# Hybrid decoder layer: the normalised attention output in a tile of its own, and GpSimd's product with the PSUM copy first of five

## The chip, the cores and the metric

The kernel runs on one core of one Trainium2 chip. The metric is the device time of one execution in microseconds. Three runs of the kernel before gave 1129.52, 1127.29 and 1125.67 us; the median is 1127.29 us.

## The reference

One decoder layer on x (1024 positions, 1024 columns, float32): one input projection into 3072 columns, four heads of differential attention, a gated short convolution, an output projection, layer norm, a gated feed-forward block with 2816 hidden columns, and a second layer norm. The change lies in what ends each attention head:

```python
a = p[:, :, 0] - lam * p[:, :, 1]                  # two causal softmaxes, in 128-query blocks
o = jnp.einsum('bhqk,bhkd->bhqd', a.astype(vt.dtype), vt)
...
o = o * lax.rsqrt(jnp.mean(jnp.square(o), axis=-1, keepdims=True) + RMS_EPS)
o = o * attn_norm_g.astype(jnp.float32) * (1.0 - lam_init)
...
cat = jnp.concatenate([attn_out, conv_out], axis=-1)
return jnp.einsum('bsc,cd->bsd', cat, w_out)
```

## The kernel before

Products that need float32 accuracy are split: a cast `hi` on ScalarE (line 63), the rest `lo = src - hi` on VectorE (line 64), and three matmuls on TensorE (lines 72 to 74). After the value projection the attention runs head by head, `attention(h)` for h = 0 to 3. Each head projects its q and k, then goes over four chunks c of 256 queries, each with two blocks `qi` of 128 queries, so block i = 2c + qi has (i + 1) x 128 keys. A block has, for each of the two softmaxes, score matmuls (lines 441 to 443), the row maximum on VectorE (line 444) and the exponential on ScalarE (line 448), and then the combination of the two (line 456 on ScalarE, line 457 on VectorE). `spread` of that block comes in the program at the start of the next block: it transposes the weights (line 408), splits them into `pa`, and after the second block of a chunk multiplies them with v into the PSUM tile `o`, which line 419 copies into `osb` on ScalarE.

`normalise` for a chunk comes one block later still, at `RMS_AT` (c, 1), after the exponentials of that block; for the last chunk of a head it comes in the next head, or after the last head. It squares `osb` on VectorE, splits the square into `sqh` and `sql`, takes the mean over the head's 128 rows with two matmuls against `ones` into `mq`, makes y = (mean square + eps)^(-1/2) on ScalarE (logarithm and exponential), and refines and applies it in five GpSimd operations: two products, a scale-and-add with the columns `gm` and `gp`, and two more products. The last writes over `osb`, and SP's queue sends `osb` to `cat_d[h]` in DRAM, from where the output projection reads it after the four heads.

All tiles of `normalise` come from the pool `at`, in which a tag without a count has one buffer. `sq` and `me` share the tag "sq", `sql` and `y` the tag "sql"; `sqh` and `osb` have tags of their own. A tile that takes a buffer waits until the tile before it in that buffer has been used for the last time.

Each head is followed in the program by parts of the short convolution (`conv_1` to `conv_3`, lines 481 to 501), whose projections (tiles X and Z, `a`, `s`, `w`, `u`) have nothing to do with the attention and fill its gaps. The order in which an engine's queue holds its instructions is not that of the source: it is laid down when the kernel is built, by a planner that gives each engine, among the instructions whose operands and buffers it takes to be ready, the one that stands first in the program. On the chip each queue runs in that order, and an instruction whose semaphore has not come holds up all behind it in its queue.

Of the kernel before, what the change touches and what calls it, by code (L numbers as in the profile page):

```python
# [8 lines left out]
F32 = mybir.dt.float32  # L9
# [3 lines left out]
ALU = mybir.AluOpType  # L13
# [3 lines left out]
P = 128  # L17
# [11 lines left out]
QC = 256  # L29
# [17 lines left out]
def layer_kernel(ctx: ExitStack, tc: tile.TileContext, x, xt, w_in, w_v, lam, vecs, w_out, ln, w_up, w_down, out):  # L47
    nc = tc.nc
    V, A, T, G = nc.vector, nc.scalar, nc.tensor, nc.gpsimd
    SQ = nc.sync  # L50

    def pool(name, stack=None, side=None, space=None, **kw):
        args = dict(name=name, bufs=1, reuse_waits="tile")
        if space is not None:
            args["space"] = space
        if side is not None:
            args["side"] = side
        return (stack or ctx).enter_context(tc.tile_pool(**args))

    def split(hi, lo, src, scale=None, eng=None):  # L60

        if scale is None:
            A.copy(hi, src)  # L63
            (eng or V).tensor_tensor(lo, src, hi.bitcast(F32), op=ALU.subtract)  # L64
        else:
            A.mul(hi, src, scale)
            V.scalar_tensor_tensor(lo, src, scale, hi.bitcast(F32), op0=ALU.mult, op1=ALU.subtract)
# [79 lines left out]
    cat_d = [dram.tile([P, S], F32, name=f"cat_d{k}") for k in range(8)]  # L147
# [172 lines left out]
    at = pool("at", ab, side="right")  # L320
# [30 lines left out]
    def normalise(h, c, osb):  # L351
        sq = at.tile([P, QC], F32, name="sq", tag="sq")
        V.tensor_tensor(sq, osb, osb, op=ALU.mult)
        sqh = at.tile([P, QC], F32R, name="sqh", tag="sqh")
        sql = at.tile([P, QC], F32R, name="sql", tag="sql")
        split(sqh, sql, sq)
        mq = p_pv.tile([P, 512], F32, name="mq", tag="pv", bufs=1)
        T.matmul(mq[:, :QC], ones, sqh, start=True, stop=False)
        T.matmul(mq[:, :QC], ones, sql, start=False, stop=True)

        me = at.tile([P, QC], F32, name="me", tag="sq")
        A.activation(me, mq[:, :QC], AF.Identity, bias=epsc)
        y = at.tile([P, QC], F32, name="y", tag="sql")
        A.activation(y, me, AF.Ln)
        A.activation(y, y, AF.Exp, scale=-0.5)  # L365
        G.tensor_tensor(me, me, y, op=ALU.mult)  # L366
        G.tensor_tensor(me, me, y, op=ALU.mult)
        G.tensor_scalar(me, me, gm, gp, op0=ALU.mult, op1=ALU.add)
        G.tensor_tensor(y, y, me, op=ALU.mult)
        G.tensor_tensor(osb, y, osb, op=ALU.mult)  # L370
        SQ.dma_start(cat_d[h][:, c * QC:(c + 1) * QC], osb)

    def attention(h):

# [27 lines left out]
        def spread(c, qi, pm, pa):  # L402
            i, nkb = 2 * c + qi, 2 * c + 2
            for j0 in range(0, i + 1, 4):
                nj = min(4, i + 1 - j0)
                tp = p_tr.tile([P, 4, P], F32, name="tp", tag="tr", bufs=1)
                for j in range(nj):
                    T.transpose(tp[:, j, :], pm[0][:, (j0 + j) * P:(j0 + j + 1) * P], ident)
                g = pa[j0 // 4]
                split(g[:, 0, 0:nj, qi * P:(qi + 1) * P], g[:, 1, 0:nj, qi * P:(qi + 1) * P], tp[:, :nj, :])  # L410
            if qi == 0:
                return
            o = p_pv.tile([P, 512], F32, name="o", tag="pv", bufs=1)
            for j in range(nkb):
                qs = slice(P if j == nkb - 1 else 0, QC)
                mm3(o[:, qs], vh[:, j, :], vl[:, j, :], pa[j // 4][:, 0, j % 4, qs], pa[j // 4][:, 1, j % 4, qs],
                    j == 0, j == nkb - 1, skip_group_check=True)
            osb = at.tile([P, QC], F32, name="osb", tag="osb")
            A.copy(osb, o[:, :QC])
            rms.append(lambda: normalise(h, c, osb))  # L420
# [272 lines left out]
    def operand(src, which, i, tail=False, eng=None):  # L693
        if tail and not (which == "T" and i < HK - NTAIL + RT):
            v = ep.tile([P, 2, 512], F32R, name=f"{which}{i}", tag="ra", bufs=NF - NKEEP)
        else:
            v = e0.tile([P, 2, 512], F32R, name=f"{which}{i}", tag="ring", bufs=RING[0])
        split(v[:, 0, :], v[:, 1, :], src, eng=eng)
        return v
# [121 lines left out]
    def add(x_, y_, op, out=None):  # L821
        if out is None:
            out = ep.tile([P, 512], F32, name="tm", tag="r", bufs=4)
        V.tensor_tensor(out, x_, y_, op=op)
        return out
# [33 lines left out]
    for j in range(HK + 2):  # L859
        if j < HK:  # L860
            op = ready.pop(0) if ready else (operand(a11[j], "S", j), operand(b11[j], "T", j))
            for t in range(4):
                mm_row(X, op, t, j == 0, j == HK - 1)
        if j >= 2:
            i = j - 2
            op = (operand(add(a21[i], a22[i], ALU.add), "S", i),
                  operand(add(b12[i], b11[i], ALU.subtract), "T", i))
# [91 lines left out]
```

## Time and profile before

| what | value |
|---|---|
| median of three runs | 1127.29 us |
| the profiled execution's own time | 1129.07 us |
| its span, first to last instruction | 1127.3 us |
| mean granted TensorE clock | 0.991 |
| TensorE matmul busy | 1084.9 us, 96% |
| VectorE busy | 906.4 us, 80% |
| ScalarE busy | 522.5 us, 46% |
| GpSimd busy | 147.6 us, 13% |
| chain that ended last: PE, DVE, ACT, POOL, DMA | 71%, 15%, 5%, 3%, 3% |

Engines are named as the profile names them: PE is TensorE's matmuls, PEld its weight loads, DVE VectorE, ACT ScalarE, POOL GpSimd, SP the queue that issues the transfers. A matmul's recorded end is modelled, and matmuls overlap, so a busy PE is not yet PE at its peak. The four heads take the span from about 85 to 380 us.

### The profile page before, as it was taken

What the parts mean: (1) busy time and instruction counts of PE and PEld (TensorE: products, weight loads), DVE (VectorE), ACT (ScalarE), POOL (GpSimd) and SP (SyncE); (2) the same over time, 40 slices, a digit from 0 to 9 for tenths busy, and PEclk for the clock granted to TensorE, in tenths of its full rate; (3) what the DMA queues carried; (4) which work ended last, traced back from release to release, by engine and by line L of the source; (5) the groups of instructions that cost most, each with busy time, mean ns of one, the idle gap of its engine ahead of it and who ended that gap; (6) DMA issues with size and microseconds to landing.
All of it is one profiled execution on the core that took longest, in us unless ns stands there. A gap on an engine that the chain in (4) does not pass through costs nothing.

```text
span 1127.3 us, 13854 instructions
## 1 busy us (share of the span) xinstructions
PE 1084.9 (96%) x4940; PEld 873.8 (78%) x4940; DVE 906.4 (80%) x1393; ACT 522.5 (46%) x980; POOL 147.6 (13%) x182
## 2 busy tenths in 40 slices
PE   7999999999999999879999999999999999999996
PEld 6777877876768888668888888888888887788885
DVE  7678898689787688998967676777777599997797
ACT  6357586386675333445433334333333333444540
POOL 0002213013031224760000000000000000000102
PEclk9999999999999999999999999999999999999998
DMA  7421201301206754423232212131312295111111
GB/s 267 150 94 43 85 25 52 115 21 52 75 29 197 279 177 159 154 75 113 94 112 70 99 59 109 57 113 57 112 56 93 78 383 220 38 66 38 46 67 75
DMA packets 50421, 118.53 MB, mean 105 GB/s; under 512 B 5040, under 2 KB 18480, under 8 KB 50352
## 3 DMA queue, kind: packets, MB, share of 16 engines
q1 hardware_dynamic: 50352, 117.64, 29.7%
q8 instruction: 39, 0.64, 0.2%
q14 instruction: 30, 0.25, 0.1%
HBM read 90.88 MB, written 26.74 MB: 104 GB/s over the span
## 4 chain that ended last, share of the span: by engine, by line
PE 71%; DVE 15%; ACT 5%; POOL 3%; DMA 3%; issue 2%; SPq 0%; POOLq 0%; DVEq 0%; ACTq 0%
PE X L74 8%; PE X L72 8%; PE X L73 8%; PE Z L74 5%; PE Z L73 5%; PE Z L72 5%; PE dx L73 2%; PE dx L74 2%; PE dx L72 2%; PE op L74 2%; PE op L73 2%; PE op L72 2%; DVE a L64 2%; PE dz L74 2%; PE dz L72 2%
## 5 line engine op out<-in xcount | busy, mean ns | idle before, releaser
L64 DVE TENSOR_TENSOR a<-s,a 128x512 fp32r<-128x512 f32 x118 | 85.3, 724 | 45.3 <-ACT a L63 44.3
L63 ACT CAST a<-s 128x512 fp32r<-128x512 f32 x118 | 73.3, 623 | 94.5 <-PE X L74 43.0
L63 ACT CAST a<-w 128x512 fp32r<-128x512 f32 x106 | 65.9, 623 | 87.3 <-PE X L74 40.4
L64 DVE TENSOR_TENSOR a<-w,a 128x512 fp32r<-128x512 f32 x102 | 72.3, 710 | 22.6 <-ACT a L63 22.2
L63 ACT CAST T<-b 128x512 fp32r<-128x512 f32 x66 | 40.6, 621 | 68.4 <-PE dz L74 33.9
L73 PE MATMUL dx<-T,S 128*128 128x512 f32 x176 | 69.0, 392 | 1.2 <-DVE T L64 1.2
L74 PE MATMUL dx<-T,S 128*128 128x512 f32 x176 | 68.5, 389 | 0.0
L72 PE MATMUL dx<-T,S 128*128 128x512 f32 x176 | 66.0, 391 | 0.0
L64 DVE TENSOR_TENSOR T<-b,T 128x512 fp32r<-128x512 f32 x66 | 45.0, 685 | 16.3 <-ACT T L63 16.3
L74 PE MATMUL op<-wo,cl 128*128 128x512 f32 x128 | 51.2, 400 | 3.2 <-DVE cl L64 3.2
L444 DVE TENSOR_REDUCE nm<-sc 128x1 f32<-128x128 f32 (+5 forms) x64 | 47.5, 750 | 7.7 <-PE sc L443 7.3
L709 POOL MEMSET gs<- 128x2 f32 x22 | 2.2, 99 | 379.6 <-DVE t L728 379.6
L73 PE MATMUL dz<-T,S 128*128 128x512 f32 x132 | 51.8, 393 | 0.0
L74 PE MATMUL dz<-T,S 128*128 128x512 f32 x132 | 51.5, 390 | 0.0
L72 PE MATMUL op<-wo,ch 128*128 128x512 f32 x128 | 51.3, 401 | 0.0
L448 ACT ACTIVATE p<-sc,nm 128x128 f32<-128x128 f32 (+5 forms) x64 | 47.6, 745 | 7.2 <-DVE p L457 4.1
L73 PE MATMUL op<-wo,ch 128*128 128x512 f32 x128 | 50.8, 397 | 0.0
L72 PE MATMUL dz<-T,S 128*128 128x512 f32 x132 | 48.4, 393 | 0.5 <-ACT T L63 0.5
L729 ACT ACTIVATE t<-t 128x1024 f32<-128x1024 f32 x22 | 23.4, 1062 | 51.9 <-DVE t L728 51.9
L441 PE MATMUL sc<-k,q 128*128 128x512 f32 (+2 forms) x96 | 37.1, 394 | 7.1 <-ACT p L448 6.1
L366 POOL TENSOR_TENSOR me<-me,y 128x256 f32<-128x256 f32 x16 | 12.5, 783 | 236.0 <-ACT y L365 236.0
L63 ACT CAST wo<-wo_r 128x512 fp32r<-128x512 f32 x40 | 24.4, 619 | 40.9 <-PE op L74 37.8
(314 smaller groups left out, 3374.9 us busy)
## 6 DMA issues: line engine op xcount, KB each, us to landing
w<-in_w_up SPq DMA_DIRECT2D x44, 512.0 KB, 3.2
b<-in_w_down SPq DMA_DIRECT2D x44, 256.0 KB, 6.9
w<-in_w_in SPq DMA_DIRECT2D x20, 512.0 KB, 3.4
wo_r<-in_w_out SPq DMA_DIRECT2D x20, 512.0 KB, 4.8
act_d<-act SPq DMA_DIRECT2D x19, 512.0 KB, 2.6
ra<-act_d SPq DMA_DIRECT2D x19, 512.0 KB, 7.0
v_d<-vs SPq DMA_DIRECT2D x16, 256.0 KB, 2.7
vhl<-v_d SPq DMA_DIRECT2D x8, 512.0 KB, 4.6
```

Source lines behind the costliest of these rows:

```text
L63: A.copy(hi, src)
L64: (eng or V).tensor_tensor(lo, src, hi.bitcast(F32), op=ALU.subtract)
L72: T.matmul(ps, lh, rh, start=first, stop=False, **kw)
L73: T.matmul(ps, lh, rl, start=False, stop=False, **kw)
L74: T.matmul(ps, ll, rh, start=False, stop=last, **kw)
L366: G.tensor_tensor(me, me, y, op=ALU.mult)
L441: T.matmul(sc[:, bs], q2[m][:, qs], k2[m][:, bs], start=True, stop=False)
L444: V.tensor_reduce(nm[:, m:m + 1], sc[:, :n], axis=AX.X, op=ALU.max, negate=True)
L448: A.activation(pt[:, :n], sc[:, :n], AF.Exp, bias=nm[:, m:m + 1], accum_out=sm[:, m:m + 1])
L709: G.memset(gs[:, 0:2], 0.0)
L729: A.activation(t_, t_, AF.Silu)
```

## The change

`normalise` gets one more tile, `on`, in the buffer of tag "sqh". The product of `y` with `osb` is made first, into `on`; the refinement of `me` follows; the last product multiplies `on` with `me`, and `on` is what is sent to DRAM. The count of operations is the same, and so are the kinds; the scale-and-add, third of the five before, is now the fourth. `osb` is read for the last time by the first GpSimd operation, `y` by the third, `me` by the fifth.

```diff
         A.activation(y, y, AF.Exp, scale=-0.5)
+        on = at.tile([P, QC], F32, name="on", tag="sqh")
+        G.tensor_tensor(on, y, osb, op=ALU.mult)
         G.tensor_tensor(me, me, y, op=ALU.mult)
         G.tensor_tensor(me, me, y, op=ALU.mult)
         G.tensor_scalar(me, me, gm, gp, op0=ALU.mult, op1=ALU.add)
-        G.tensor_tensor(y, y, me, op=ALU.mult)
-        G.tensor_tensor(osb, y, osb, op=ALU.mult)
-        SQ.dma_start(cat_d[h][:, c * QC:(c + 1) * QC], osb)
+        G.tensor_tensor(on, on, me, op=ALU.mult)
+        SQ.dma_start(cat_d[h][:, c * QC:(c + 1) * QC], on)
```

## Rows read from the trace of the kernel before

**Rows 1.** The page: busy us of each engine, share of the span, instructions.

```profile
PE 1084.9 (96%) x4940; PEld 873.8 (78%) x4940; DVE 906.4 (80%) x1393; ACT 522.5 (46%) x980; POOL 147.6 (13%) x182
```

**Rows 2.** Chain that ended last, in head 0: start us, duration us, what.

```profile
99.48 0.75 POOL me L366
...
104.70 1.87 DMA cat_d<-osb
```

**Rows 3.** Waits of ScalarE, 85 to 380 us: total us, times, longest.

```profile
ACT osb L419 <- DMA cat_d<-osb: 7.7, 5, 2.0
```

**Rows 4.** Timeline, ScalarE: start, duration us, instruction, [idle before <- releaser].

```profile
106.65 0.37 ACT L419 COPY osb<-o 128x256 f32<-128x256 f32 x1 [1.57 <-DMA cat_d<-osb]
...
108.07 0.41 ACT L63 CAST sqh<-sq 128x256 fp32r<-128x256 f32 x1
...
174.26 0.37 ACT L419 COPY osb<-o 128x256 f32<-128x256 f32 x1 [2.00 <-DMA cat_d<-osb]
...
258.66 0.37 ACT L419 COPY osb<-o 128x256 f32<-128x256 f32 x1 [1.00 <-DMA cat_d<-osb]
259.53 0.40 ACT L63 CAST sqh<-sq 128x256 fp32r<-128x256 f32 x1 [0.49 <-DVE sq L353]
...
329.61 0.37 ACT L419 COPY osb<-o 128x256 f32<-128x256 f32 x1 [1.96 <-DMA cat_d<-osb]
```

**Rows 5.** Timeline, TensorE, behind those copies.

```profile
108.24 0.50 PE L441 MATMUL sc<-k,q 128*128 128x512 f32 x1 [0.74 <-ACT p L448]
...
130.50 0.39 PE L73 MATMUL o<-pa,vhl 128*128 128x256 f32 x1 [0.72 <-DVE pa L64]
...
176.38 0.50 PE L441 MATMUL sc<-k,q 128*128 128x512 f32 x1 [1.61 <-ACT p L448]
...
259.99 0.39 PE L358 MATMUL mq<-sqh,ones 128*128 128x256 f32 x1 [0.58 <-ACT sqh L63]
...
331.72 0.50 PE L441 MATMUL sc<-k,q 128*128 128x512 f32 x1 [1.56 <-ACT p L448]
```

**Rows 6.** VectorE in head 0 (timeline), and busy us by stretch (windows).

```profile
107.22 0.29 DVE L64 TENSOR_TENSOR pa<-tp,pa 128x128 fp32r<-128x128 f32 x1 [1.32 <-ACT pa L63]
107.43 0.41 DVE L353 TENSOR_TENSOR sq<-osb 128x256 f32<-128x256 f32 x1
...
108.82 0.42 DVE L64 TENSOR_TENSOR sql<-sq,sqh 128x256 fp32r<-128x256 f32 x1
...
110.00:130.00 20.00, 19.79 (x113) 16.18 (x111) 19.94 (x30) 13.76 (x27) 9.05 (x11) 1.00 0.04 14
```

**Rows 7.** Timeline, head 0: last matmul into `o`, ScalarE's idle stretch.

```profile
100.08 0.27 PE L74 MATMUL o<-pa,vhl 128*128 128x128 f32 x1
...
103.60 0.59 ACT L63 CAST pa<-tp 128x512 fp32r<-128x512 f32 x1 [1.60 <-PE tp L408]
```

**Rows 8.** Timeline, VectorE and GpSimd side by side, heads 0, 1 and 2.

```profile
101.30 0.68 DVE L64 TENSOR_TENSOR a<-w,a 128x512 fp32r<-128x512 f32 x1
101.47 1.58 POOL L368 TENSOR_SCALAR me<-me,gm,gp 128x256 f32<-128x256 f32 x1
101.90 0.88 DVE L457 SCALAR_TENSOR_TENSOR p<-p,cc,p 128x640 f32<-128x640 f32 x1
...
169.11 1.20 POOL L368 TENSOR_SCALAR me<-me,gm,gp 128x256 f32<-128x256 f32 x1
169.12 0.92 DVE L457 SCALAR_TENSOR_TENSOR p<-p,cc,p 128x640 f32<-128x640 f32 x1
...
254.11 0.56 POOL L368 TENSOR_SCALAR me<-me,gm,gp 128x256 f32<-128x256 f32 x1
254.75 0.73 POOL L369 TENSOR_TENSOR y<-y,me 128x256 f32<-128x256 f32 x1
254.81 1.35 DVE L457 SCALAR_TENSOR_TENSOR p<-p,cc,p 128x640 f32<-128x640 f32 x1
```

**Rows 9.** Timeline, TensorE, head 2: the transposes behind L457.

```profile
256.31 0.63 PE L408 MATMUL tp<-ident,p 128*128 128x128 f32 x4 [0.72 <-DVE p L457]
```

## The prediction

> **What bounds the kernel now.** I read the page's busy times first: TensorE is at work for 96% of the span, ScalarE for 46% [rows 1]. A change on ScalarE, VectorE or GpSimd therefore gains only what takes idle time from TensorE. Next I read the chain of waits over the four attention heads (about 85 to 380 us), since only `normalise` is touched. In each head it passes once through all five GpSimd products and the transfer behind them: in head 0 from 99.48 us to the landing at 104.70 + 1.87 = 106.57 us [rows 2]. So the edited place is on the path four times. Third, who waited there: ScalarE stood 7.7 us, five times, at the copy of `o` into `osb` for that transfer [rows 3]. Four of these are the second chunk of each head, 1.57, 2.00, 1.00 and 1.96 us, 6.53 in all; the fifth is the rest, some 1.1 us [rows 4]. Fourth, what TensorE lost by it, read from TensorE's rows just behind these places: it was idle 0.74, 1.61 and 1.56 us for an exponential of L448 that stood behind the copy, and 0.58 us for the cast into `sqh`, 4.49 us together [rows 5]. In the stretch after the first of them TensorE is full (19.79 of 20 us), with VectorE at 19.94 [rows 6]; time won on the other engines there is not won in the span, unless VectorE's backlog itself stops TensorE, as it does once (0.72 us at 130.50) [rows 5].
>
> **Part 1, `osb` becomes free earlier.** Before, the next copy into `osb` had to wait for five products and the transfer. Now it waits for the first product: 99.48 + 0.75 = 100.23 us in head 0 [rows 2]. The last product of the matmuls that it copies ends at 100.35 [rows 7]. So the copy can go at once, and ScalarE has an idle stretch of 1.60 us just there, before 103.60 [rows 7] (heads 1 and 3 have one like it): the copy's 0.37 us lie in it, cost nothing, and would cost 0.37 us of ScalarE if that cover were gone.
>
> **Part 2, what takes its place.** `on` lies in the one buffer of tag `sqh`. The next chunk's cast into `sqh` must now wait until `on` has been read by its transfer, which lands when it did before: five products, the same transfer, 106.57 us. As the rows stand, the cast ran at 108.07, 1.50 us after that landing [rows 4], and with that order it would never wait. But the cast stands there only because `sq` waited for the late `osb`. With `osb` early, `sq` can run on VectorE as soon as `me`, whose buffer it takes, is read for the last time (just ahead of the transfer's issue at 104.70 [rows 2], one product later than before), and VectorE has 1.32 us idle before 107.22 [rows 6]. The order of each queue is laid down before the run, by when the planner thinks that an operand or buffer is ready. It put the copy into `osb` behind the second exponential of the head's sixth block, that is, at the time at which it thought that the transfer would be in, and it was too early by the 1.57, 2.00, 1.00 and 1.96 us that ScalarE then stood. The cast into `sqh` now depends on the same transfer and ranks ahead of the next block's exponential, so I expect it at that same place. The added wait is then worth between nothing (the cast stays behind the landing) and 2.00 us a head; I take the old waits, since the row of the old copy is the nearest. Behind the cast in the queue stand a cast of `pa` and the next exponential of L448, and TensorE's score matmul at 108.24 waits for that one, as before [rows 5]. In heads 0, 1 and 3 a cast of 0.41 us stands where a copy of 0.37 us stood, and the three gaps of TensorE (0.74, 1.61, 1.56) stay: nothing gained.
>
> Two things are gained. In head 2 TensorE waited 0.58 us for the cast itself, which came 0.87 us behind the copy (259.53 against 258.66) [rows 4, 5]; the cast now stands in the copy's place, and the gap goes: -0.58. In head 0 VectorE works without a break from 107.22 until it stops TensorE at 130.50; `sq` and `sql` (0.41 and 0.42 us) leave that stretch for the idle time ahead of it, more than the gap of 0.72 [rows 5, 6]: -0.72. Sum -1.30. Bounds for the two together: nothing, if other work slips in, and -1.30.
>
> **Part 3, the order of the five products.** It was product, product, scale-and-add, product, product; it becomes product, product, product, scale-and-add, product. No instruction is added on GpSimd, VectorE, SP or the DMA queues; `on` itself waits for no one, since the matmuls that read `sqh` are over before `y` can be made; `y` is free two products earlier, which nobody waits for. What changes is which of them stands beside VectorE's combination of the two softmaxes (L457), for which TensorE's transposes wait. On 640 columns it took 0.88 and 0.92 us beside the scale-and-add (heads 0 and 1; head 3 is like head 1), and 1.35 us beside two products (head 2) [rows 8]; the scale-and-add, in turn, took 1.58 and 1.20 us there, against 0.56 ahead of L457 in head 2. In head 2 the third product will be over when L457 starts (254.11 + 0.73 = 254.84 against 254.81), and the scale-and-add stands beside it: 1.35 falls to about 0.90, and the transposes' gap of 0.72 us with it [rows 8, 9]: -0.45. In head 1 the third operation and L457 start within 0.01 us of each other (169.11 and 169.12), and in head 3 alike. If the product goes first, L457 ends later by about a product, 0.73 us, and TensorE with it, 1.46 in both; if L457 goes first, nothing. I take the middle, +0.73, as no row decides. In head 0 another two-operand instruction of VectorE (101.30) runs directly ahead of L457 while GpSimd already stands, so I put nothing there. Part 3: +0.28, between -0.45 and +1.01.
>
> The Trainium skill (GPSIMD Engine Reference, 1. Specifications) says that GpSimd shares its SBUF interfaces with VectorE, and that the two contend where VectorE's instruction has two SBUF inputs or runs in a 2-port mode. It speaks against this change, which moves a two-input product to where L457 runs. It does not say which side waits; if VectorE did in heads 0, 1 and 3, at the 0.45 us by which the rows of L457 differ, part 3 would be 3 x 0.45 - 0.45 = +0.90 and the whole -0.4 us. The rows bear out that there is contention, and that the scale-and-add, not VectorE, stood in those three heads.
>
> **Sum.** -1.30 + 0.28 = -1.0 us. The profiled execution took 1129.07 us (span 1127.3 and 1.8 around it), so it would take 1128.1. It is 1.78 us above the median of the runs, 1127.29; applied to the median, 1126.3 us.
>
> **Rivals.** *A, the forecast: the wait moves to the cast into `sqh`.* 1126.3; its own range is 1123 to 1130, since a new order of ScalarE's and VectorE's queues also moves fill work of the convolution projections by a few tenths of a microsecond in each of some ten places. Chance 0.48.
>
> *B, the wait is gone.* The cast into `sqh` is put behind the exponential, as it stands in heads 0, 1 and 3 now, and the transfer has landed by then. All four gaps go: -4.49, then -0.72 in head 0 and +0.28 from part 3: -4.9, or 1122.4. For it: the 1.50 us between landing and cast today. Against: the cast's rank ahead of that exponential. Chance 0.28.
>
> *C, slower: VectorE stands too.* The buffer of `sq` is now given back by the fifth product instead of the fourth, and the planner's view of the products is too short by what contention adds (5.22 us from 99.48 to 104.70, where five at 0.73 would be 3.65) [rows 2, 8]. If `sq` is put ahead of the next block's reduction and of a `pa` subtraction, these, and the transposes that wait for `pa`, stand behind it. At most VectorE would stand as long as ScalarE did, 6.53 us over the heads; about half lies beside ScalarE's own wait. Price +3.3, 1130.6 (at most 1133.8). It decides from where `sq` reaches the head of VectorE's queue before 104.70. Against: VectorE is seldom idle earlier. Chance 0.18.
>
> *D, nothing changes.* The planner keeps its order and what moves is hidden behind TensorE: 1127.3. For it: TensorE's 96%. Against: the copy ranks first where it is ready. Chance 0.06.
>
> **How the numbers follow.** 0.3% is 3.4 us, about what a measurement of this kernel tells from no change: faster means below 1123.9, slower above 1130.7. Faster: 0.27 of B and 0.04 of A's tail, 0.31. Slower: 0.12 of C and 0.08 of A's and D's tails, 0.20. Same: 0.49. The range takes in B with a microsecond and a half below it and C to its price: 1120.8 to 1131.0.
>
> **What would show it.** Right: the four waits of `osb` for a transfer are gone, and ScalarE stands 1 to 2 us at the cast into `sqh` for the transfer of `on`, once a head, with TensorE's gaps of 0.7 to 1.6 us still behind it. B: neither wait, and no such gaps. C: VectorE idle ahead of `sq`, released by GpSimd's last product. Part 3: L457 on 640 columns at 0.9 us in head 2, and its length in heads 1 and 3. The prediction is wrong if the copy into `osb` does not move, if the cast meets no wait, or if stretches after 380 us change.

## The result and the profile after

| | before | changed |
|---|---|---|
| median, six runs each | 1126.65 us | 1134.72 us |
| profiled execution, its span | 1129.07, 1127.3 us | 1135.76, 1134.0 us |
| first score matmul to first matmul of the output projection | 288.6 us | 295.6 us |

The ratio is 1.0058, 95% interval 1.0042 to 1.0073: slower by 0.6%, or 6.5 us (8.1 between the two medians), outside the range that was forecast. All of it arises in the four heads, 7.0 us there against 6.7 in the span of the profiled executions. The page of the changed kernel (its first lines and the shares of its chain) shows TensorE busy for 4.9 us longer with the same 4940 instructions, and GpSimd for 5.9 us longer [rows 1]. It does not say why: its row of the clock has 9 tenths in every slice.

```profile
span 1134.0 us, 13870 instructions
## 1 busy us (share of the span) xinstructions
PE 1089.8 (96%) x4940; PEld 878.9 (78%) x4940; DVE 902.4 (80%) x1393; ACT 522.7 (46%) x980; POOL 153.5 (14%) x182
...
PE 71%; DVE 13%; ACT 5%; DMA 4%; POOL 3%; issue 2%; SPq 0%; POOLq 0%; DVEq 0%; ACTq 0%
```

The waits of the heads in the changed kernel (total us, times, longest) show the forecast mechanism. `osb` waits for no transfer any more, only for its own matmuls [rows 3]; the cast into `sqh` does wait for one, four times, once a head. TensorE now stands behind that cast itself, and VectorE stands at `sq` for the fifth product.

```profile
ACT sqh L63 <- DMA cat_d<-on: 8.4, 4, 2.5
ACT osb L420 <- PE o L74: 7.6, 4, 2.4
...
PE mq L358 <- ACT sqh L63: 7.0, 4, 2.1
...
DVE sq L353 <- POOL on L371: 3.8, 4, 1.1
```

Head 1 in the changed kernel, ScalarE's timeline: the copy goes at 169.63, 4.6 us earlier than before [rows 4], in what had been idle time, and the cast then stands 2.49 us.

```profile
169.63 0.36 ACT L420 COPY osb<-o 128x256 f32<-128x256 f32 x1
169.88 0.60 ACT L63 CAST pa<-tp 128x512 fp32r<-128x512 f32 x1
172.97 0.40 ACT L63 CAST sqh<-sq 128x256 fp32r<-128x256 f32 x1 [2.49 <-DMA cat_d<-on]
```

TensorE's timeline at the same place. Its queue has one matmul of the fill work after the scores, and then the product of `sqh`: 2.07 us idle. Read the starts behind it: from 174.31 to 174.73 one 512-column matmul takes 0.42 us, from 177.54 to 177.77 it takes 0.23.

```profile
170.88 0.47 PE L73 MATMUL Z<-xb_22l,a 128*128 128x512 f32 x1
173.43 0.39 PE L358 MATMUL mq<-sqh,ones 128*128 128x256 f32 x1 [2.07 <-ACT sqh L63]
...
174.31 0.63 PE L72 MATMUL Z<-xb_22h,a 128*128 128x512 f32 x1
174.73 0.63 PE L73 MATMUL Z<-xb_22l,a 128*128 128x512 f32 x1
...
177.54 0.40 PE L74 MATMUL Z<-xb_22h,a 128*128 128x512 f32 x1
177.77 0.40 PE L72 MATMUL X<-xb_t3h,a 128*128 128x512 f32 x1
```

The windows of that stretch (PE, PEld, DVE, ACT, POOL busy; the third column from the right is the granted clock) say why: behind the idle stretch the clock is at 0.50 of 2.4 GHz, that is 1.2 GHz, while TensorE is busy throughout.

```profile
168.00:171.30 3.30, 3.18 (x20) 2.19 (x18) 2.18 (x4) 2.18 (x5) 2.91 (x2) 1.00 0.10 38
171.30:173.40 2.10, 0.06 (x1) 0.00 (x0) 0.75 (x2) 0.40 (x1) 0.00 (x0) 1.00 0.67 133
174.00:177.20 3.20, 3.20 (x10) 2.62 (x9) 3.09 (x5) 2.76 (x6) 0.00 (x0) 0.50 0.15 58
178.00:181.00 3.00, 3.00 (x18) 2.50 (x17) 2.46 (x4) 2.39 (x5) 1.88 (x3) 1.00 0.00 0
```

The kernel before had its gap of 1.61 us at this place [rows 5], and its windows show the clock at full speed on both sides:

```profile
174.70:176.40 1.70, 0.09 (x2) 0.03 (x1) 1.44 (x4) 1.70 (x5) 0.00 (x0) 1.00 0.59 239
176.40:180.00 3.60, 3.60 (x19) 2.95 (x20) 3.46 (x6) 3.15 (x6) 0.71 (x1) 1.00 0.00 0
```

The same happens in heads 2 and 3 of the changed kernel (idle 2.12 and 2.04 us, clock low from 262.6 and 334.3):

```profile
262.64:266.05 3.41, 3.33 (x9) 2.71 (x10) 3.35 (x7) 2.78 (x7) 0.00 (x0) 0.50 0.28 111
334.32:337.73 3.41, 3.41 (x9) 2.67 (x9) 2.65 (x6) 2.32 (x7) 0.00 (x0) 0.50 0.00 0
```

In head 0 the gap is 0.75 us and the clock stays.

### The profile page after: what moved, and what is told of

The parts are those of the page before. It is cut to its first block, busy times and chain, and to the rows that moved or that the text cites. A ratio compares the mean times of both kernels' runs of the same rounds, so it can differ in the third digit from the quotient of the medians.

```text
span 1134.0 us, 13870 instructions
## 1 busy us (share of the span) xinstructions
PE 1089.8 (96%) x4940; PEld 878.9 (78%) x4940; DVE 902.4 (80%) x1393; ACT 522.7 (46%) x980; POOL 153.5 (14%) x182
## 4 chain that ended last, share of the span: by engine, by line
PE 71%; DVE 13%; ACT 5%; DMA 4%; POOL 3%; issue 2%; SPq 0%; POOLq 0%; DVEq 0%; ACTq 0%
PE X L72 8%; PE X L74 8%; PE X L73 8%; PE Z L74 5%; PE Z L73 5%; PE Z L72 5%; PE dx L73 2%; PE dx L74 2%; PE dx L72 2%; PE op L74 2%; PE op L72 2%; PE op L73 2%; DVE a L64 2%; PE dz L74 2%; PE dz L72 2%
## 5 line engine op out<-in xcount | busy, mean ns | idle before, releaser
L64 DVE TENSOR_TENSOR a<-s,a 128x512 fp32r<-128x512 f32 x118 | 83.0, 705 | 44.4 <-ACT a L63 43.3
L367 POOL TENSOR_TENSOR on<-y,osb 128x256 f32<-128x256 f32 x16 | 14.6, 911 | 242.3 <-ACT y L365 200.6
```

What stands on the lines that cost most here:

```text
L367: G.tensor_tensor(on, y, osb, op=ALU.mult)
```

## The stage's account

The windows from the first score matmul to the first matmul of the output projection, one row each of the kernel before, the changed one, and two of the experiments (e3, a buffer of its own for `on`; e4, more matmuls in the gap):

```profile
81.00:369.60 288.60, 276.94 (x1422) 216.61 (x1423) 239.27 (x418) 194.32 (x419) 63.78 (x78) 1.00 0.21 72
```

```profile
80.20:375.80 295.60, 281.85 (x1422) 221.98 (x1423) 234.66 (x418) 194.76 (x419) 69.23 (x78) 0.98 0.21 71
```

```profile
79.60:359.60 280.00, 276.06 (x1423) 217.25 (x1424) 234.95 (x418) 193.60 (x419) 67.89 (x78) 1.00 0.23 75
```

```profile
80.30:379.70 299.40, 285.46 (x1446) 222.38 (x1447) 236.60 (x418) 195.15 (x419) 67.95 (x78) 1.00 0.21 69
```

TensorE's idle time is the length less its busy time: 11.7 us before, 13.8 changed. TensorE's busy time grew from 276.9 to 281.9 us for the same 1422 matmuls; 2.1 + 4.9 are the 7.0. In the changed kernel 10.2 us of the stage ran at 1.2 GHz, where 512-column matmuls followed each other at 0.42 us instead of 0.23, so nearly half of that, at most 5.1 us, is lost: that is the growth of the busy time. The same account for all kernels of this study, length and idle time from the kernel's own window row, the time at 1.2 GHz from the stretches that its trace shows at a clock of 0.50:

| kernel | length | idle | at 1.2 GHz | length - idle - half of that |
|---|---|---|---|---|
| before | 288.6 | 11.7 | 0 | 276.9 |
| changed | 295.6 | 13.8 | 10.2 | 276.7 |
| e1 order only | 291.7 | 13.5 | 3.4 | 276.5 |
| e2 tile only | 292.3 | 13.5 | 3.4 | 277.1 |
| e3 own buffer | 280.0 | 3.9 | 0 | 276.1 |
| e4 keep busy | 299.4 | 13.9 | 0 | 285.5, with 24 matmuls more |
| e5 square in PSUM | 288.1 | 9.0 | 6.8 | 275.7 |
| e6 two of osb | 282.3 | 6.4 | 0 | 275.9 |
| e7 own buffer, old order | 287.7 | 10.0 | 3.4 | 276.0 |
| e8 keep one | 296.5 | 13.9 | 6.8 | 279.2, with 6 matmuls more |
| e9 before, square in PSUM | 303.6 | 18.9 | 17.1 | 276.2 |
| e10 buffers exchanged | 294.4 | 14.7 | 6.8 | 276.3 |
| e11 on in sql's buffer | 288.6 | 11.0 | 0 | 277.6 |

The last column is TensorE's busy time less half of the time at 1.2 GHz. Apart from e4 and e8, whose added matmuls are in it, it is the same within 2 us, while the lengths differ by 24. So TensorE's idle time and the time at 1.2 GHz are what the stage's length is made of; where VectorE, ScalarE or GpSimd wait counts only as far as it makes these.

## The experiments

All times are medians, ratios are against the kernel before on the same chip (medians 1127.3 to 1127.7 us).

**e1, the order alone.**

```diff
+        G.tensor_tensor(osb, y, osb, op=ALU.mult)
         G.tensor_tensor(me, me, y, op=ALU.mult)
...
-        G.tensor_tensor(y, y, me, op=ALU.mult)
-        G.tensor_tensor(osb, y, osb, op=ALU.mult)
+        G.tensor_tensor(osb, osb, me, op=ALU.mult)
```

> The kernel before (1126.7 us) with the first product ahead of the refinement, but in place: it writes over osb, the last product too, and osb is sent. No new tile. Theory W (the loss of 8 us is the wait of the cast into sqh for the transfer of on, once a head, with what it does to TensorE): osb waits for the transfer as before, no cast into sqh waits, 1125 to 1129. Theory O (the loss is the new order of the products beside VectorE's two-operand instructions): most of the loss is here too, 1131 to 1135. Theory P (any new order of the queues costs it): undecided, anything between.

Measured 1131.02 us, ratio 1.0032 (1.0019 to 1.0044): at the lower end of O's range and outside W's, with 3.6 us of loss, about half of what the change lost. The trace shows the slower instructions that O had put down. VectorE's combination of the softmaxes (L457) took 1.34 and 1.37 us in heads 0 and 1, for 0.88 and 0.92 before, and 1.37 in head 3; in head 2 the scale-and-add took 2.22 us for 0.56 [rows 8], and ScalarE then stood 2.80 us for the transfer behind it, for 1.00 [rows 4]:

```profile
ACT osb L419 <- DMA cat_d<-osb: 13.6, 6, 4.0
...
101.66 1.34 DVE L457 SCALAR_TENSOR_TENSOR p<-p,cc,p 128x640 f32<-128x640 f32 x1
...
169.65 0.74 POOL L368 TENSOR_TENSOR me<-me,y 128x256 f32<-128x256 f32 x1
169.69 1.37 DVE L457 SCALAR_TENSOR_TENSOR p<-p,cc,p 128x640 f32<-128x640 f32 x1
...
256.32 2.22 POOL L369 TENSOR_SCALAR me<-me,gm,gp 128x256 f32<-128x256 f32 x1
261.38 0.37 ACT L419 COPY osb<-o 128x256 f32<-128x256 f32 x1 [2.80 <-DMA cat_d<-osb]
```

The whole wait for the transfer was 7.7 us before [rows 3]; the clock fell once in the stage, behind 2.39 us idle in head 2. What the planner's new order of the queues adds to this was not separated.

**e2, the tile alone.**

```diff
-        G.tensor_tensor(osb, y, osb, op=ALU.mult)
+        on = at.tile([P, QC], F32, name="on", tag="sqh")
+        G.tensor_tensor(on, y, osb, op=ALU.mult)
```

> The kernel before with only the target of the last product changed: it goes to on, in the buffer of tag sqh, and on is sent; the products keep their old order, so osb is free after the fifth product, not the first. Theory W: the cast into sqh is held by the same landing, but the copy into osb comes only 1.9 us ahead of it, so the cast waits 0.5 to 2 us and TensorE loses 0 to 2 us at mq in each head: 1127 to 1134, slower where a clock stretch at half speed shows behind such a gap. Theory O: the order is the old one, so 1125 to 1128. Theory P: undecided.

1132.94 us, 1.0045 (1.0031 to 1.0058), in the range of W, but for the most part not by W's way: the cast waited for the transfer three times, 0.8 us at most. ScalarE stood 3.6 us once at `osb` for the fifth product, and the clock fell once in the stage, behind the 2.45 us that TensorE then stood in head 0:

```profile
104.50 0.37 ACT L420 COPY osb<-o 128x256 f32<-128x256 f32 x1 [3.57 <-POOL on L371]
105.82 0.50 PE L442 MATMUL sc<-k,q 128*128 128x512 f32 x1 [2.45 <-ACT p L449]
```

Either part alone loses; the two losses do not add up (3.6 + 5.1 against 6.5 from the ratios).

**e3, a buffer of its own for `on`.** The room for it comes from the raw square, put into the unused half of the bank of `mq`; the tags of `me` and `y` move up.

```diff
+        mq = p_pv.tile([P, 512], F32, name="mq", tag="pv", bufs=1)
+        sq = mq[:, QC:]
...
-        me = at.tile([P, QC], F32, name="me", tag="sq")
+        me = at.tile([P, QC], F32, name="me", tag="sql")
...
-        y = at.tile([P, QC], F32, name="y", tag="sql")
+        y = at.tile([P, QC], F32, name="y", tag="sqh")
...
-        on = at.tile([P, QC], F32, name="on", tag="sqh")
+        on = at.tile([P, QC], F32, name="on", tag="on")
```

> The changed kernel (1134.7 us) with a buffer for on that nobody else takes. The room for it comes from the raw square, which goes to the unused half of the PSUM tile mq; me then takes the buffer of sql, y that of sqh. Theory W: neither osb nor sqh waits for a transfer, TensorE is not idle 2 us ahead of mq, its clock keeps 2.4 GHz through the four heads, 1120 to 1125, below the kernel before. Theory O: the order of the products is that of the changed kernel, so 1131 to 1135. Theory P: anything, most likely above 1127.

1117.57 us, 0.9917 (0.9903 to 0.9930): better than W expected, and the fastest kernel of the study, 0.8% below the kernel before. Theory O by itself is out: the products stand in the order of the changed kernel, and the scale-and-add of head 2 takes 2.23 us here too, but no write waits for its transfer. Head 1 in its timeline: the cast and the product of `sqh` follow without a wait.

```profile
169.66 0.33 SPq L372 DMA_DIRECT2D cat_d<-on  x1
...
170.19 0.38 ACT L63 CAST sqh<-mq 128x256 fp32r<-128x256 f32 x1
...
171.74 0.28 PE L358 MATMUL mq<-sqh,ones 128*128 128x256 f32 x1
```

The cast begins 0.53 us behind the issue of the transfer; in the changed kernel it had to wait until that had landed.

**e4, matmuls into the gap.**

```diff
+        if c == 1:
+            for _ in range(3):
+                T.matmul(mq[:, :QC], ident, sq, start=True, stop=True)
```

> The changed kernel with three matmuls more (ident times the raw square, into mq, thrown away) ahead of the first matmul into mq, in the second chunk of each head only, that is, in the gap of TensorE. The wait for the transfer stays. They take 1.3 us a head where there is no gap. Theory W with the clock as half of the loss: the gap falls below 1 us, the clock stays at 2.4 GHz in heads 1 to 3, and about 1.7 us a head come back: 1128 to 1131. If the clock were without weight and only the wait counted: no change or slower, 1134 to 1138. Theories O and P: 1134 to 1140.

1137.47 us, 1.0093 (1.0079 to 1.0106): a miss of the forecast gain, and a time in the range put down for a clock without weight, so the time alone does not speak for the clock. The clock did stay at 2.4 GHz in all four heads (table), but the added matmuls took 285.5 - 276.7 = 8.8 us of TensorE, not the 5.2 that I had put (3 a head became 24 records of some 0.4 us), and TensorE's idle time stayed as it was, 13.9 us for 13.8. -5.1 + 8.8 = +3.7, and the stage grew by 3.8: the account holds, with the clock in it at the price worked out above.

**e5, the control: the square in PSUM, the wait kept.** e3 with the changed kernel's tags of `me`, `y` and `on`.

> The control for the buffer of its own (1117.6 us): the raw square goes to PSUM as there, but on stays in the buffer of tag sqh, as in the changed kernel. Theory W: the wait of the cast for the transfer is back, 1.5 to 2.5 us in each head, with TensorE idle ahead of mq and its clock falling: 1130 to 1136. If the gain of the other kernel came from the square in PSUM (theory S): 1116 to 1121.

1127.26 us, 0.9991 (0.9980 to 1.0002): a miss for W as I had put it. The wait is there, and longer than in the changed kernel:

```profile
ACT sqh L63 <- DMA cat_d<-on: 9.7, 5, 3.2
```

But TensorE stood long behind it in two heads only, 0 and 2 (2.89 and 1.80 us, each with a fall of the clock, where the cast waited 3.17 and 2.61 us). In heads 1 and 3 the cast waited 1.25 and 1.31 us, and TensorE stood 0.52 and 0.59: the wait is half of the changed kernel's there, and more of the fill work stands ahead of `mq` in its queue. So the wait in sum is not the loss; its length in each head and what TensorE has left to do during it decide, and the two were not separated. By the ratios, of the 15.9 us between the changed kernel and e3, 7.6 came with the square in PSUM and 8.3 with the buffer of its own (and the tags of `me` and `y` that go with it).

**e6, two buffers of `osb`, the old order.** The room is made as in e3.

```diff
-            osb = at.tile([P, QC], F32, name="osb", tag="osb")
+            osb = at.tile([P, QC], F32, name="osb", tag="osb", bufs=2)
```

> The kernel before with two buffers for osb and nothing moved in the order of the products; the room comes from the raw square in PSUM, me in the buffer of sql, y in that of sqh. Theory W: no instruction waits for a transfer of the attention output, 1116 to 1121, as with the buffer of its own. Theory O (part of what was gained is that GpSimd's product with osb comes first): 1121 to 1126.

1120.16 us, 0.9937 (0.9923 to 0.9951): W. No instruction waits for a transfer of the attention output.

**e7, the buffer of its own, the old order of the products.** e3 with `on` made last, from `y` and `osb`.

> The buffer of its own for on, but with the products in the order of the kernel before: osb is free after the fifth product. Theory W: no wait for a transfer; the copy into osb may wait for the fifth product, up to 1.5 us in a head: 1117 to 1123. Theory O in the sense that the new order costs 3.6 us, as it did in place: 1114 to 1116. The other way round (the new order helps once the buffer is free): 1119 to 1124.

1125.37 us, 0.9976 (0.9964 to 0.9987), by the ratios 6.6 us above e3: with the buffer free, the new order helps, the third of the cases put down, and by a little more than its range. ScalarE waits for the fifth product instead of a transfer:

```profile
ACT osb L420 <- POOL on L371: 9.9, 4, 2.8
```

**e8, one matmul into the gap, in heads 1 to 3.**

```diff
+        if c == 1 and h > 0:
+            T.matmul(mq[:, :QC], ident, sq, start=True, stop=True)
```

> The changed kernel (1134.7 us) with a single matmul more (ident times the raw square, thrown away) ahead of the first into mq, in the second chunk of heads 1 to 3, the three places where the clock fell. It adds 0.5 us a head where there is no gap, and lies in the gap of 2 us here. The wait for the transfer stays. Theory W with the clock: no stretch at 1.2 GHz in heads 1 to 3, 3 x 1.7 us come back less at most 1.5: 1129.5 to 1132. If a fall of the clock costs nothing (what is lost is made up behind it): 1134 to 1136.

1134.84 us, 1.0062 (1.0046 to 1.0078): no gain, and again a time in the range put down for a clock without weight. The gap was split (0.67 and 1.26 us in head 1), and the clock fell all the same in heads 1 and 3, but not in head 2. By the account, one fall less gives back 1.7 us and the added matmuls take 2.5, with the idle time as it was: +0.9 in all, which is what the stage grew. Two of its windows, behind the gaps of heads 1 and 2:

```profile
174.00:177.00 3.00, 3.00 (x10) 2.48 (x11) 2.97 (x7) 1.85 (x4) 0.00 (x0) 0.50 0.35 143
...
264.60:267.60 3.00, 3.00 (x16) 2.34 (x15) 3.00 (x6) 2.65 (x6) 0.00 (x0) 1.00 0.15 60
```

**e9, the kernel before with the square in PSUM.**

> The kernel before (1127.7 us) with only the raw square moved to PSUM; osb is still sent and held by its transfer, in one buffer. It is the control for two buffers of osb (1120.2). Theory W: the copy into osb waits for the transfer as before, 6 to 8 us in all; the square in PSUM is not what counts: 1124 to 1129. Theory S (the square in PSUM, which frees the buffer that me holds until the fourth product, gains by itself, as it did on the changed kernel): 1118 to 1122.

1138.66 us, 1.0099 (1.0080 to 1.0119): slower than either theory had it; on this kernel theory S is out. ScalarE's wait for the transfer is three times as long, and the stage has five stretches' worth of 3.4 us at 1.2 GHz (table). Why the square in PSUM makes that wait longer here, and gained on the changed kernel (e5), was not found. With two buffers of `osb`, and `me` and `y` moved up a tag, the same kernel is e6, 18 us faster.

```profile
ACT osb L419 <- DMA cat_d<-osb: 22.6, 7, 4.8
```

**e10, `me` and `y` exchange buffers.**

```diff
-        me = at.tile([P, QC], F32, name="me", tag="sq")
+        me = at.tile([P, QC], F32, name="me", tag="sql")
...
-        y = at.tile([P, QC], F32, name="y", tag="sql")
+        y = at.tile([P, QC], F32, name="y", tag="sq")
```

> The changed kernel (1134.7 us) with the buffers of me and y exchanged: me lies in that of sql, y in that of sq, so the raw square waits for the third GpSimd operation and not for the fifth. The wait of the cast for the transfer stays. Theory H (of the loss that the square in PSUM took away, 7.5 us, most is VectorE standing at the raw square for the fifth product, 3.8 us in four waits): those waits go, 1127 to 1130. Theory W: VectorE's wait lies inside that of the cast, which ends at the landing anyway, so TensorE's gap of 2 us ahead of mq stays: 1132 to 1136.

1133.38 us, 1.0049 (1.0031 to 1.0067), which can't be told from the changed kernel. VectorE's wait for the fifth product is gone, the cast's is not (8.9 us), and TensorE stands 0.89, 2.20, 2.26 and 2.19 us ahead of `mq`. Theory H is out.

**e11, the transfer holds the buffer of `sql`.**

```diff
-        y = at.tile([P, QC], F32, name="y", tag="sql")
+        y = at.tile([P, QC], F32, name="y", tag="sqh")
-        on = at.tile([P, QC], F32, name="on", tag="sqh")
+        on = at.tile([P, QC], F32, name="on", tag="sql")
```

> The changed kernel with on in the buffer of sql and y in that of sqh: the transfer holds up the buffer that the next chunk needs last, on VectorE, and no longer the one of ScalarE's cast. Theory W: ScalarE's 8.4 us of waiting for the transfer go; VectorE waits at the low part instead, 4 to 8 us in all, and TensorE one matmul later: 1127 to 1134. If the place of the wait did not matter, only the landing: 1133 to 1136.

1126.39 us, 0.9991 (0.9982 to 1.0001): two tags take back the whole loss, and the time falls just below the range that was put down. The landing comes as late behind the first product as in the changed kernel, but the buffer that it holds is written 1.5 us behind `sqh` (170.47 and 171.97 us in head 1), and on VectorE, which waits 0.93 us for it. TensorE's gap falls into two, with `sqh`'s product, a matmul of the fill work and a transpose between them, and the clock does not fall in the heads:

```profile
170.93 0.39 PE L358 MATMUL mq<-sqh,ones 128*128 128x256 f32 x1 [0.59 <-ACT sqh L63]
...
172.45 0.39 PE L359 MATMUL mq<-sql,ones 128*128 128x256 f32 x1 [0.79 <-DVE sql L64]
```

## Why the prediction was wrong

**Part 1 held.** The copy into `osb` moved into ScalarE's idle time and waits for no transfer.

**Part 2 held in its mechanism and failed in its price.** That "the wait moves to the cast into `sqh`" is what the trace shows, four times: 0.93, 2.49, 2.54 and 2.46 us, where at most 2.00 a head had been put. The step that failed is "the three gaps of TensorE (0.74, 1.61, 1.56) stay: nothing gained", and with it "the gap goes: -0.58" in head 2. They became 0.75, 2.07 and 2.04, and head 2's became 2.12: 6.98 us for 4.49. The rows show two reasons.

The first is the landing, which was put "when it did before: five products, the same transfer". In heads 1 to 3 the scale-and-add took 2.22 to 2.23 us, where it had taken 1.20, 0.56 and 1.20, and all that hangs on the fifth product came later by it. The chain from the first product to the write that the transfer held up (the copy before, the cast now), in us:

| head | chain before | chain changed | gap before | gap changed |
|---|---|---|---|---|
| 0 | 7.17 | 7.00 | 0.74 | 0.75 |
| 1 | 7.15 | 7.62 | 1.61 | 2.07 |
| 2 | 6.47 | 7.65 | 0.58 | 2.12 |
| 3 | 7.10 | 7.58 | 1.56 | 2.04 |

In heads 1 and 3 the gap grew by as much as the chain. The first products of heads 1 and 3 before, and then the rows of the changed kernel:

```profile
167.11 0.75 POOL L366 TENSOR_TENSOR me<-me,y 128x256 f32<-128x256 f32 x1 [11.29 <-ACT y L365]
...
322.51 0.74 POOL L366 TENSOR_TENSOR me<-me,y 128x256 f32<-128x256 f32 x1 [11.28 <-ACT y L365]
```

```profile
165.35 0.97 POOL L367 TENSOR_TENSOR on<-y,osb 128x256 f32<-128x256 f32 x1 [11.56 <-ACT y L365]
...
167.83 0.87 DVE L458 SCALAR_TENSOR_TENSOR p<-p,cc,p 128x640 f32<-128x640 f32 x1
167.94 2.23 POOL L370 TENSOR_SCALAR me<-me,gm,gp 128x256 f32<-128x256 f32 x1
...
171.02 0.33 SPq L372 DMA_DIRECT2D cat_d<-on  x1
...
325.19 0.96 POOL L367 TENSOR_TENSOR on<-y,osb 128x256 f32<-128x256 f32 x1 [11.53 <-ACT y L365]
...
332.77 0.40 ACT L63 CAST sqh<-sq 128x256 fp32r<-128x256 f32 x1 [2.46 <-DMA cat_d<-on]
```

The second is the place. I carried over the old gaps because the old copy and the new cast stand at the same place on ScalarE, and did not ask what stood behind them on TensorE. Before, in head 1, TensorE still had matmuls until 174.77 (176.38 less 1.61), half a microsecond past the start of the copy at 174.26 [rows 4, 5]; now it has none from 171.36, 1.6 us ahead of the cast at 172.97, since the product of `sqh` comes next in its queue. With the chain at its old length, the table would give about the old gaps of heads 1 and 3 again (an estimate: 2.07 less 0.47, and 2.04 less 0.48). That would have been luck, since the idle stretch lies at another place. e11 shows that the place counts: its chain is as long (7.63 us in head 1), and no gap at these places is above 0.83 us. No run has the changed kernel's cast with the old length of the chain, so how much of the loss is the chain's stays open.

**The larger error is a term that was not there.** Idle time was priced as idle time. Behind three of the four gaps TensorE's clock was at 1.2 GHz for 10.2 us in all, worth 4.9 of the 7.0 us; e3, e6 and e11, without such a fall in the heads, are all below or level with the kernel before (e4 has none either, and is slower by its added matmuls). The gain of 0.72 us at 130.50 in head 0 did come: that gap is gone.

**Part 3 was right in size for L457, and left out its other side.** The rows of the changed kernel in heads 0 and 2 (head 1 is shown above, and head 3 is like it):

```profile
100.71 1.12 POOL L369 TENSOR_TENSOR me<-me,y 128x256 f32<-128x256 f32 x1
101.17 1.34 DVE L458 SCALAR_TENSOR_TENSOR p<-p,cc,p 128x640 f32<-128x640 f32 x1
...
257.08 0.87 DVE L458 SCALAR_TENSOR_TENSOR p<-p,cc,p 128x640 f32<-128x640 f32 x1
257.20 2.22 POOL L370 TENSOR_SCALAR me<-me,gm,gp 128x256 f32<-128x256 f32 x1
```

In head 2 the combination fell from 1.35 to 0.87 us, as put [rows 8], and the transposes' gap of 0.72 went [rows 9]. In heads 1 and 3 L457 went first, for which "nothing" was put: it took no longer, so the +0.73 did not come, but the scale-and-add beside it took 2.23 us, and that is the longer chain of the table. In head 0, where I had put nothing, the combination took 1.34 beside the third product for 0.88 [rows 8]; its gap grew from 1.01 to 1.46. The contention that I had cited from the Trainium skill (GPSIMD Engine Reference, 1. Specifications) is in the trace on both sides: VectorE stood in head 0, GpSimd's scale-and-add, 2.22 to 2.23 us long, in heads 1 to 3. In place (e1) it was VectorE in heads 0, 1 and 3, by 0.45 us each, as the prediction had worked out beside that citation. The order cost 3.6 us in place, and gained 6.6 us once `on` had its own buffer (e3 against e7).

**The rivals.** C's mechanism came true beside A's: VectorE stands at `sq` for the fifth product, 3.8 us in four. e10 takes that wait away and nothing is won, since it lies inside the cast's wait. So C's wait has no part in the loss that could be measured, and the loss is about twice C's price. B, the wait gone, is what e3 and e6 do; they are faster than the 1122.4 that I had put for it, because with no transfer in the way more gaps close than the four that I had listed (idle 3.9 us for 11.7).

**Open.** Why one matmul in the gap saved the clock in head 2 and not in heads 1 and 3 (e8) was not found. The clock's share is shown by the account of thirteen kernels and by e4's balance, not by a kernel in which it alone was changed. A buffer of its own for `on` with the square left in SBUF was not run, so what the square in PSUM does in e3 apart from making room was not separated.

## What to carry to other kernels

When a result is sent from a buffer that later work shares, ask which of the next writes needs that buffer first, and what TensorE still has in its queue when that write stands; a buffer of its own for what is sent, with the room made for it, was worth 16 us against the changed kernel (9.4 against the one before), and the mere choice of the shared buffer 7.6. Count the engine that stands as well as the one that is slowed: an instruction of GpSimd that stands beside VectorE moves all that waits for its result. Price a gap of TensorE twice: the idle time, and the stretch behind it at the lower clock if it is one that brings the clock down. And in a kernel whose queues a planner fills, an edit that frees a buffer earlier pulls all that depended on it forward, up to the next thing that is held.

## What the runs showed of the hardware

TensorE's clock fell in the middle of dense work, with TensorE at work before and behind. In the four heads it fell behind single idle stretches of 2.07, 2.12 and 2.04 us (changed kernel), 2.39 (e1), 2.45 (e2), 2.89 and 1.80 (e5), 2.07 (e7), 2.67, 2.41, 2.08 and 2.47 (e9), 2.20 and 2.19 (e10), and twice behind two shorter ones close together (e8: 0.67 and 1.26, 0.67 and 1.19). It stayed at 2.4 GHz behind 1.61 and 1.56 (before) and 1.77 and 1.50 (e1), but also behind 2.26 in head 2 of e10, 2.30 in e9, and 0.68 and 1.31 in head 2 of e8. So the length of the gap alone does not settle it. Each time some 3.4 us passed at 1.2 GHz (6.8 the last time in e9), in which 512-column matmuls followed each other at 0.42 us instead of 0.23. A fall cost 1.6 to 1.7 us beside a gap of about 2 (4.9 us for three), and a busy TensorE at half speed counts as busy, 281.9 us for 276.9 in the same stage.

VectorE's combination of the softmaxes and GpSimd's operations hold each other up, and in most of these rows the one that started later stood. In e1, head 1, a product started at 169.65 and the combination at 169.69: the product took 0.74 us, the combination 1.37. In the changed kernel, head 1, the combination started at 167.83 and the scale-and-add at 167.94: the combination took 0.87, the scale-and-add 2.23. Where the two starts lie 0.01 us apart, in head 1 before, the scale-and-add stood, though its recorded start is the earlier one [rows 8].
